# Two small constant tiles moved from the front of SBUF to a place between activations and weight halves

## The chip, the cores and the metric

The kernel runs on one core of a Trainium2 chip. The metric is the device time of one launch in microseconds, as the median of several runs. Inside the core the work is done by TensorE (PE for its matmuls, PEld for its loads of stationary operands), VectorE (DVE), ScalarE (ACT) and GpSimd (POOL), while DMA queues bring the weights from HBM into SBUF, the on-chip memory.

## The reference

The reference is a two-layer decoder trunk over 256 tokens of width 2048, in float32. Layer 0 mixes with multi-head latent attention beside a causal pooling mixer, layer 1 with a gated short convolution, and each layer ends in a squared-ReLU MLP of hidden width 8192:

```python
for layer in range(DEPTH):                     # DEPTH = 2
    h = _rmsnorm(x, mix_norm_g[layer])
    if layer % 2 == 0:
        c_q, c_kv, k_rope, u_pool = jnp.split(h @ even_w_in[e], split_at, axis=-1)
        a = _mla(c_q, c_kv, k_rope, ...)       # 8 heads, causal softmax
        b = _pool_mixer(u_pool, ...)           # trailing means over 2/4/8/16 tokens
        x = x + jnp.concatenate([a, b], axis=-1) @ even_w_out[e]
    else:
        x = x + _short_conv(h, odd_w_in[o], odd_conv_w[o], odd_w_out[o])
    x = x + _mlp(_rmsnorm(x, mlp_norm_g[layer]), w_mlp_up[layer], w_mlp_down[layer])
```

`_mlp(h, w_up, w_down)` is `square(relu(h @ w_up)) @ w_down`.

## The kernel before, in words

**Split operands.** Each float32 matrix product is made of three products of a reduced type: a weight or activation is split into a high part (`hi`) and a low part (`lo`), and `lo * lo` is left out. Weights arrive in blocks of 1 MB (`raw`, 128 partitions by 2048 elements, DMA at L129). `halved` (L132) makes the halves from each block, two tiles of 1024 elements at a time: ScalarE copies `hi` (L141), VectorE subtracts it from the block to give `lo` (L142). Six slots of `hi` and six of `lo` go round.

**Two orders of operands.** TensorE loads one operand first and keeps it (the stationary operand, `lhsT`), then streams the other (the moving operand, `rhs`). The kernel uses both orders:

```python
def columns_out(o, act, kt, w, c0, first, last):          # weights stationary
    hi, lo = w
    nc.tensor.matmul(o, lhsT=hi[:, c0:c0 + P], rhs=act[:, kt, :], start=first, stop=False)          # L161, 512 wide
    nc.tensor.matmul(o[:, S:2 * S], lhsT=lo[:, c0:c0 + P], rhs=act[:, kt, 0:S], start=False, stop=last)  # L162, 256 wide
```

`columns_out` makes the MLP's up projection and the convolution's three gates; its moving operand is always `xT`, the normed activations of the layer. `tokens_out` (L147 to L156) is the other way round: the stationary operand is an activation tile (`hT`, or `xT` in the latent projection at the start) and the moving one a weight half, `hi` at L154, `lo` at L155, `hi` at L156, 512 wide nearly everywhere, 384 and 320 in the latent projection. The lines L777 to L779 inside `down_seven` do the same for a part of the MLP's down projection; their stationary operand is a piece of `hT` or of `fT`, a tile of sums of such pieces. `columns_summed` (L167 to L169) serves the pooling mixer with steps of 256, weights stationary, `xT` moving.

**Stages.** In order: latent and pooling projections and attention of layer 0 (to about 240 us), the MLP of layer 0, the convolution layer (from about 960 us: the gates L911 to L948, all in `columns_out`, then `project_out`), the MLP of layer 1. An MLP starts with two chunks of up projection by themselves. Then `mlp` interleaves up steps with down products in an order written out by hand (L883), fourteen chunks of up projection among seven groups of products, and ends with four blocks of down projection alone (L889). In all there are 2816 pairs of L161 and L162: 768 in the gates, 256 in the opening chunks of the two MLPs, 1792 in the interleaved parts. There are 880 triples of L154 to L156 that are 512 wide, and 392 triples of L777 to L779, of which 168 have `hT` stationary and 224 `fT`.

**Where tiles lie in SBUF.** Pools get their places one after the other from the front, in the order in which the code opens them: `const`, `big` (`x`, `xT`, `qkv`), `small`, `acts` (four activation tiles `hT`), `halves` (twelve slots), then the pools of the stage (`raws`, and `blocks`, `forms` or `conv`). The pool `attn` lies at the far end. All sizes below are bytes in each partition; every tile is rounded up to 32 bytes. In the program before:

| tiles | start of the first | size of one | start modulo 256 |
|---|---|---|---|
| `gains`, `minus_half`, `warm`, `ident` (in `const`) | 16512, 17024, 17152, 17280 | 512, 128, 128, 512 | |
| `x` | 18208 | 16384 | 32 |
| `xT` | 34592 | 32768 | 32 |
| `hT` (four) | 78048 | 8192 | 224 |
| `hi` (six), `lo` (six) | 110816 | 4352 | 224 |
| `raw` (three) | 163040 | 8192 (8704 at first) | 224 |
| `fT` (two) | 204000 | 8192 | 224 |

A slot of `halves` is 4352 bytes, seventeen times 256, so all twelve start at the same place modulo 256 and alternate modulo 512. Inside the tiles the pieces used by matmuls start at multiples of 512 bytes, or of 1024 in `hT`.

**The two tiles of the change.** `minus_half` is 32 columns of -0.5, written once by GpSimd (L248) and read by GpSimd's few power operations (L269, L367, L564, L915). `warm` takes the result of one ScalarE activation (L250) that is there to have the activation table loaded early; nothing reads it.

Of the kernel before, what the change touches and what calls it, by code (L numbers as in the profile page):

```python
# [9 lines left out]
F32 = mybir.dt.float32  # L10
F32R = mybir.dt.float32r
I32 = mybir.dt.int32
AF = mybir.ActivationFunctionType
# [3 lines left out]
P = 128  # L17
# [50 lines left out]
def trunk(ctx: ExitStack, tc, x_in, xT_in, gains_in, pos_in, w_up, w_down, w_in, pool_in, w_uq, w_ukv,  # L68
          qn_g, kn_g, pool_w, w_out, odd_in, odd_out, freq_in, out):
    nc = tc.nc  # L70
    PSUM = bass.MemoryType.PSUM

    const = ctx.enter_context(tc.tile_pool(name="const", bufs=1))
# [14 lines left out]
    small = ctx.enter_context(tc.tile_pool(name="small", bufs=2))  # L88
    T4 = dict(tag="t", bufs=4)
    acts = ctx.enter_context(tc.tile_pool(name="acts", bufs=4))  # L90
    pools = dict(halves=ctx.enter_context(tc.tile_pool(name="halves", bufs=6)))
    psum = ctx.enter_context(tc.tile_pool(name="psum", bufs=4, space=PSUM))

# [150 lines left out]
    for name, n in (("mix0", KD), ("mix1", KD), ("mlp", 2 * KD), ("conv", 3 * KD), ("scale", POOLW // P), ("qa", KL), ("kva", KL)):  # L244
        gains[name] = (gains_t, at)
        at += n
    minus_half = const.tile([P, 32], F32, name="minus_half")
    nc.gpsimd.memset(minus_half, -0.5)  # L248
    warm = const.tile([P, 32], F32, name="warm")
    nc.scalar.activation(warm, minus_half, AF.Square)  # L250
    ident = const.tile([P, P], F32, name="ident")
    make_identity(nc, ident)
    ps_warm = bank2()
# [751 lines left out]
```

## Time and profile before

| | |
|---|---|
| median of 3 runs | 2018.85 us (2018.52 to 2019.94) |
| the profiled execution's own time | 2020.08 us |
| its span, first to last instruction | 2018.3 us |
| mean granted TensorE clock | 0.998 |
| PE busy | 2007.2 us, 99% |
| DVE, ACT, POOL busy | 1394.9, 1122.2, 96.4 us |
| read from HBM | 455.89 MB |

A row of the timeline starts with the time at which an instruction began, counted from the start of the span. For matmuls the time from one start to the next is the step that TensorE took; the duration in the second column is longer, since matmuls are pipelined, and does not count here. Below, a step is always taken as the time between two starts with many steps between them, divided by their number, since starts are shown to 0.01 us.

### The profile page before, as it was taken

What the parts mean: (1) busy time and instruction counts of PE and PEld (TensorE: products, weight loads), DVE (VectorE), ACT (ScalarE), POOL (GpSimd) and SP (SyncE); (2) the same over time, 40 slices, a digit from 0 to 9 for tenths busy, and PEclk for the clock granted to TensorE, in tenths of its full rate; (3) what the DMA queues carried; (4) which work ended last, traced back from release to release, by engine and by line L of the source; (5) the groups of instructions that cost most, each with busy time, mean ns of one, the idle gap of its engine ahead of it and who ended that gap; (6) DMA issues with size and microseconds to landing.
All of it is one profiled execution on the core that took longest, in us unless ns stands there. A gap on an engine that the chain in (4) does not pass through costs nothing.

```text
span 2018.3 us, 26720 instructions
## 1 busy us (share of the span) xinstructions
PE 2007.2 (99%) x10532; PEld 1723.4 (85%) x10532; DVE 1394.9 (69%) x1737; ACT 1122.2 (56%) x1480; POOL 96.4 (5%) x126
## 2 busy tenths in 40 slices
PE   8999999999999999999999999999999999999999
PEld 8988888888888888888888888888888888888887
DVE  6677667777777777676566656567777777767774
ACT  6476556665556555555444444456555566555552
POOL 1330000000000000000000000000000000000000
PEclk9999999999999999999999999999999999999999
DMA  8453758787978878665555557658787977879663
GB/s 312 163 193 141 228 189 231 266 254 251 271 250 271 252 240 276 233 209 188 183 181 187 185 186 245 215 185 244 241 282 243 284 235 265 253 251 286 201 219 125
DMA packets 67006, 459.72 MB, mean 228 GB/s; under 512 B 7280, under 2 KB 9760, under 8 KB 11968
## 3 DMA queue, kind: packets, MB, share of 16 engines
q1 hardware_dynamic: 58224, 397.89, 54.5%
q0 software_dynamic: 8224, 58.94, 15.4%
q8 instruction: 82, 1.34, 0.3%
q10 hardware_dynamic: 432, 1.18, 0.2%
q14 instruction: 44, 0.36, 0.0%
HBM read 455.89 MB, written 2.10 MB: 227 GB/s over the span
## 4 chain that ended last, share of the span: by engine, by line
PE 96%; DVE 1%; POOL 1%; DMA 1%; ACT 1%; issue 0%; SPq 0%; ACTq 0%; DVEq 0%; POOLq 0%
PE ps L161 32%; PE ps L162 16%; PE ps L154 10%; PE ps L156 10%; PE ps L155 10%; PE ps L777 4%; PE ps L779 4%; PE ps L778 4%; DVE lo L142 1%; DMA raw<-in_even_w_in 1%; PE ps L289 1%; PE ps L167 0%; PE ps L169 0%; PE ps L168 0%; POOL pn L489 0%
## 5 line engine op out<-in xcount | busy, mean ns | idle before, releaser
L142 DVE TENSOR_TENSOR lo<-raw,hi 128x1024 fp32r<-128x1024 f32 (+2 forms) x694 | 847.6, 1225 | 444.4 <-ACT hi L141 443.5
L141 ACT CAST hi<-raw 128x1024 fp32r<-128x1024 f32 (+2 forms) x694 | 725.7, 1048 | 613.2 <-PE ps L161 338.1
L161 PE MATMUL ps<-xT,hi 128*128 128x512 f32 x2816 | 992.1, 394 | 0.0
L162 PE MATMUL ps<-xT,lo 128*128 128x256 f32 x2816 | 790.8, 281 | 0.0
L161 PEld LDWEIGHTS ps<-xT,hi 128*128 128x128 f32 x2816 | 529.4, 188 | 123.8
L162 PEld LDWEIGHTS ps<-xT,lo 128*128 128x128 f32 x2816 | 528.0, 188 | 3.6
L154 PE MATMUL ps<-hi,hT 128*128 128x512 f32 (+1 forms) x896 | 349.1, 390 | 0.0
L156 PE MATMUL ps<-hi,hT 128*128 128x512 f32 (+1 forms) x896 | 347.3, 388 | 0.0
L155 PE MATMUL ps<-lo,hT 128*128 128x512 f32 (+1 forms) x896 | 347.1, 387 | 0.0
L154 PEld LDWEIGHTS ps<-hi,hT 128*128 128x128 f32 x896 | 168.3, 188 | 35.0 <-issue 1.3
L156 PEld LDWEIGHTS ps<-hi,hT 128*128 128x128 f32 x896 | 168.3, 188 | 34.8
L155 PEld LDWEIGHTS ps<-lo,hT 128*128 128x128 f32 x896 | 168.4, 188 | 33.2
L141 ACT CAST hi<-t 128x1024 fp32r<-128x1024 f32 x84 | 88.5, 1053 | 92.7 <-PE ps L161 50.7
L142 DVE TENSOR_TENSOR lo<-t,hi 128x1024 fp32r<-128x1024 f32 x84 | 102.6, 1221 | 44.3 <-ACT hi L141 44.1
L767 POOL DMA_DIRECT2D t<-in_w_mlp_down x42 | 36.6, 872 | 1144.4 <-DVE lo L142 682.5
L777 PE MATMUL ps<-hi,fT 128*128 128x512 f32 x224 | 88.1, 393 | 0.0
L779 PE MATMUL ps<-hi,fT 128*128 128x512 f32 x224 | 87.7, 392 | 0.0
L778 PE MATMUL ps<-lo,fT 128*128 128x512 f32 x224 | 87.0, 389 | 0.0
L777 PE MATMUL ps<-hi,hT 128*128 128x512 f32 x168 | 65.8, 392 | 0.0
L779 PE MATMUL ps<-hi,hT 128*128 128x512 f32 x168 | 65.5, 390 | 0.0
L778 PE MATMUL ps<-lo,hT 128*128 128x512 f32 x168 | 65.4, 389 | 0.0
L867 DVE SCALAR_TENSOR_TENSOR x<-ps,r,x 128x512 f32<-128x512 f32 (+1 forms) x73 | 50.9, 737 | 14.5 <-PE ps L156 14.5
(184 smaller groups left out, 1563.9 us busy)
## 6 DMA issues: line engine op xcount, KB each, us to landing
raw<-in_w_mlp_up SPq DMA_DIRECT2D x128, 1024.0 KB, 6.4
raw<-in_w_mlp_down SPq DMA_DIRECT2D x114, 1024.0 KB, 5.2
raw<-in_odd_w_in SPq DMA_DIRECT2D x48, 1024.0 KB, 4.9
t<-in_w_mlp_down POOLq DMA_DIRECT2D x42, 1024.0 KB, 9.7
raw<-in_even_w_out SPq DMA_DIRECT2D x16, 1024.0 KB, 5.0
raw<-in_odd_w_out SPq DMA_DIRECT2D x16, 1024.0 KB, 5.0
t<-in_w_mlp_down SPq DMA_DIRECT2D x14, 1024.0 KB, 5.0
v<-in_w_mlp_down SPq DMA_DIRECT2D x14, 1024.0 KB, 4.9
```

The lines of the kernel that those rows point to most:

```text
L141: a = nc.scalar.copy(h, r)
L142: v = nc.vector.tensor_tensor(out=l, in0=r, in1=h.bitcast(F32), op=ALU.subtract)
L154: nc.tensor.matmul(o, lhsT=a_hi, rhs=hi[:, c0:c0 + n], start=first, stop=False)
L155: nc.tensor.matmul(o, lhsT=a_hi, rhs=lo[:, c0:c0 + n], start=False, stop=False)
L156: nc.tensor.matmul(o, lhsT=a_lo, rhs=hi[:, c0:c0 + n], start=False, stop=last)
L161: nc.tensor.matmul(o, lhsT=hi[:, c0:c0 + P], rhs=act[:, kt, :], start=first, stop=False)
L162: nc.tensor.matmul(o[:, S:2 * S], lhsT=lo[:, c0:c0 + P], rhs=act[:, kt, 0:S], start=False, stop=last)
L767: nc.gpsimd.dma_start(b, at(e, n), accum_op=ALU.add)
L777: nc.tensor.matmul(o, lhsT=a_hi, rhs=hi, start=q == 0, stop=False)
L778: nc.tensor.matmul(o, lhsT=a_hi, rhs=lo, start=False, stop=False)
L779: nc.tensor.matmul(o, lhsT=a_lo, rhs=hi, start=False, stop=q == 3)
L867: nc.vector.scalar_tensor_tensor(out=xb, in0=ps[:, t, :n], scalar=r2[0][:, t:t + 1], in1=xb, op0=ALU.mult, op1=ALU.add)
```

## The change

A pool `back` is opened between `acts` and `halves`, and the two tiles move there from `const`. `warm` shrinks from 32 columns (128 bytes) to 16 (64 bytes), and its activation reads 16 columns.

```diff
     acts = ctx.enter_context(tc.tile_pool(name="acts", bufs=4))
+    back = ctx.enter_context(tc.tile_pool(name="back", bufs=1))
     pools = dict(halves=ctx.enter_context(tc.tile_pool(name="halves", bufs=6)))
...
-    minus_half = const.tile([P, 32], F32, name="minus_half")
+    minus_half = back.tile([P, 32], F32, name="minus_half")
     nc.gpsimd.memset(minus_half, -0.5)
-    warm = const.tile([P, 32], F32, name="warm")
-    nc.scalar.activation(warm, minus_half, AF.Square)
+    warm = back.tile([P, 16], F32, name="warm")
+    nc.scalar.activation(warm, minus_half[:, :16], AF.Square)
```

No other instruction is added, removed or moved in the code.

## The prediction

> **What bounds the kernel now.** I read the page's busy times first, then its chain, then the waits of PE, then the starts of matmuls in the timeline, stage by stage.
>
> ```profile
> PE 2007.2 (99%) x10532; PEld 1723.4 (85%) x10532; DVE 1394.9 (69%) x1737; ACT 1122.2 (56%) x1480; POOL 96.4 (5%) x126
> PEclk9999999999999999999999999999999999999999
> DMA  8453758787978878665555557658787977879663
> PE 96%; DVE 1%; POOL 1%; DMA 1%; ACT 1%; issue 0%; SPq 0%; ACTq 0%; DVEq 0%; POOLq 0%
> ```
>
> TensorE is busy 99% of the span and is 96% of the chain that ended last. DMA, VectorE and ScalarE all have slack. The waits of PE say the same:
>
> ```profile
> PE ps L255 <- POOL ident masks.py:199: 2.5, 1, 2.5
> PE ps L154 <- ACT hi L141: 2.0, 2, 1.1
> PE ps L167 <- ACT qkv L525: 1.6, 1, 1.6
> PE ps L155 <- DVE lo L142: 1.0, 2, 0.9
> PE ps L167 <- DVE hT L205: 0.2, 1, 0.2
> ```
>
> That is 7.3 us of named waits in the whole run. So the time is the sum of matmul steps, and the change, which adds no work, can matter only if steps of matmuls get longer or shorter. What does a step take? The next rows are pairs of starts of the same line, read in order.
>
> ```profile
> 1099.71 0.39 PE L161 MATMUL ps<-xT,hi 128*128 128x512 f32 x1
> 1102.89 0.39 PE L161 MATMUL ps<-xT,hi 128*128 128x512 f32 x1
> ...
> 1600.47 0.40 PE L161 MATMUL ps<-xT,hi 128*128 128x512 f32 x1
> 1611.64 0.39 PE L161 MATMUL ps<-xT,hi 128*128 128x512 f32 x1
> ...
> 1254.77 0.39 PE L154 MATMUL ps<-hi,hT 128*128 128x512 f32 x1
> 1259.53 0.39 PE L154 MATMUL ps<-hi,hT 128*128 128x512 f32 x1
> ...
> 2008.69 0.28 PE L154 MATMUL ps<-hi,hT 128*128 128x256 f32 x1
> 2014.09 0.28 PE L154 MATMUL ps<-hi,hT 128*128 128x256 f32 x1
> ...
> 61.05 0.28 PE L167 MATMUL ps<-xT,hi 128*128 128x256 f32 x1
> 66.35 0.28 PE L167 MATMUL ps<-xT,hi 128*128 128x256 f32 x1
> ```
>
> First two rows, in the gates of the convolution: nine pairs of L161 and L162 lie between them, 3.18 us / 9 = 353.3 ns a pair. Next two, in the interleaved MLP: 32 pairs in 11.17 us, 349.1 ns a pair. Then `tokens_out` in the output projection: 21 steps in 4.76 us, 226.7 ns for a step of 512. The closing steps of 256 in the same function: 45 in 5.40 us, 120.0 ns. Last, `columns_summed`: 45 steps of 256 in 5.30 us, 117.8 ns.
>
> The reader is to see this: 226.7 + 120.0 = 346.7 ns is what a step of 512 and one of 256 cost in `tokens_out`. The same two widths in `columns_out` cost 349.1 or 353.3 ns, 2.4 or 6.6 ns more. Nothing waits there; the loads of stationary operands and the streams just run slightly slower. The granted clock is full in all four stages:
>
> ```profile
> 1000.00:1100.00 100.00, 100.00 (x568) 87.12 (x567) 62.59 (x78) 43.23 (x47) 0.41 (x4) 1.00 0.55 189
> 1400.00:1960.00 560.00, 560.00 (x2858) 476.97 (x2857) 413.11 (x476) 326.91 (x379) 19.86 (x23) 1.00 0.80 253
> 1240.00:1320.00 80.00, 80.00 (x366) 66.42 (x365) 44.64 (x48) 38.52 (x54) 1.77 (x2) 1.00 0.72 242
> 1970.00:2010.00 40.00, 40.00 (x183) 33.34 (x182) 19.99 (x21) 11.61 (x11) 0.00 (x0) 1.00 0.39 139
> ```
>
> (Columns: window, its length, busy us of PE, PEld, DVE, ACT, POOL, granted clock, DMA share, GB/s.) The slow gates have the least ACT and DVE work and a low DMA share, so other engines' traffic is not what lengthens their steps.
>
> A second place shows that a step of one width has two lengths. In the latent projection, sixteen k-tiles follow each other, each with twelve steps of 384 and six of 320:
>
> ```profile
> 13.69 0.34 PE L155 MATMUL ps<-lo,xT 128*128 128x384 f32 x1
> 14.21 0.34 PE L155 MATMUL ps<-lo,xT 128*128 128x384 f32 x1
> ...
> 46.17 0.34 PE L154 MATMUL ps<-hi,xT 128*128 128x384 f32 x1
> 48.25 0.31 PE L154 MATMUL ps<-hi,xT 128*128 128x320 f32 x1
> ...
> 49.13 0.34 PE L154 MATMUL ps<-hi,xT 128*128 128x384 f32 x1
> 51.25 0.31 PE L154 MATMUL ps<-hi,xT 128*128 128x320 f32 x1
> ```
>
> The first pair is in the first k-tile: three steps in 0.52 us, 173.3 ns. The second: twelve in 2.08 us, 173.3 ns. The third, the k-tile after it: twelve in 2.12 us, 176.7 ns. So there is a short step and a long one, 3.4 ns apart, and from about 43 us on they alternate with the k-tile.
>
> **The change part by part.** *The instructions.* One activation reads 16 columns for 32; the write of `minus_half` and all of GpSimd's power operations stay.
>
> ```profile
> L250 ACT ACTIVATE warm<-minus_half x1: 229/229/229, 2.5 to 2.5; 128x32 f32<-128x32 f32 x1
> 2.35 13.03 DMA raw<-in_even_w_in
> ```
>
> The activation takes 229 ns at 2.5 us, under the first weight load, which the chain shows from 2.35 us for 13.03 us. It is worth nothing while that load is there, and at most 0.2 us if it were gone. The change adds no wait and moves no DMA; no queue's order changes. I cost this part at 0.
>
> *The addresses.* `const` loses 256 bytes, so `x`, `xT`, `ident`, `small` and `hT` start 256 lower: the same place modulo 256. `back` gives 128 + 64 = 192 bytes back, so `hi`, `lo`, `raw`, `fT` and what follows start 64 lower: 160 modulo 256 instead of 224. Operands that are both before `back`, or both after it, keep their distance: the transposes with `ident`, VectorE's and ScalarE's passes over `raw`, `hi` and `lo`, and the 224 triples with `fT`. What alters is the distance from the moving operand to the stationary one, modulo 256, wherever one is a weight half and the other is `xT` or `hT`:
>
> - `columns_out`, weights over `xT`: 224 - 32 = 192 before, 160 - 32 = 128 after.
> - `tokens_out` and the triples with `hT`: 0 before, 224 - 160 = 64 after.
> - latent projection, `xT` over weights: 64 before (32 - 224), 128 after.
>
> This lines up with the steps. Distance 0: always the short step (226.7, 120.0). Distance 64 or 192, both odd multiples of 64: 349.1 or 353.3 ns a pair, and long steps in half of the latent k-tiles. I take as theory that the load of the next stationary operand and the running stream get in each other's way in SBUF at odd multiples of 64, and not at even ones. Two rows speak against it: 117.8 ns at distance 192 is shorter than 120.0 at 0, and the first k-tile has the short step at distance 64.
>
> *What it is worth.* In the gates and opening chunks 768 + 256 = 1024 pairs would go from 353.3 to 346.7 ns: 1024 x 6.6 = 6.8 us less. In the interleaved parts 1792 x 2.4 = 4.3 us less. The latent k-tiles with the long step: six of them, 6 x 12 x 3.4 ns = 0.2 us less. Against it, 880 x 3 + 168 x 3 = 3144 steps of 512 go to distance 64, where before shows no step of 512 at all. Bounds: 0 each (the steps of 320 of that distance, and the first k-tile, show nothing extra), and 3.4 ns each (the k-tiles with the long step), together 10.7 us; below nothing only if a step of 512 could be shorter than the 226.7 ns which all of `tokens_out` keeps, and 117.8 against 120.0 leaves that open for the 256-wide ones alone. I take the middle, since the row nearest in shape, 384 wide in the same function at the same distance, has the long step in every second k-tile, and the weight slots will again alternate modulo 512 as they do there: 1572 x 3.4 = 5.3 us more. Sum: -6.8 - 4.3 - 0.2 + 5.3 = -6.0 us. The profiled execution took 2020.08 us around a span of 2018.3; the same 6.0 comes off the median of the runs shown, 2018.85, which is 1.2 below it: 2012.9, say 2013 us.
>
> *A rule that speaks against it.* By the rows above, stages with the same granted clock and nothing awaited differ by up to 6.6 ns a pair. The Trainium skill, page "TensorE: Matmul & The Clock Gate", Part 2, "Step-by-step: what each phase is for", has TensorE read the stream and the next load through two independent SBUF ports, and "Loading the next tile's weights doesn't steal SBUF read bandwidth from the running matmul"; its page "SBUF — State Buffer", "Who interferes with whom", says "PE and ACT never wait on anyone". By that rule no address matters and the sum is 0, which is 2018.85 us. This trace fits it badly where one width has steps of 173.3 and 176.7 ns, but it shows no run with other addresses, so it cannot refute it.
>
> **The rivals.** *No change.* The length of a step hangs on how the stream of matmuls entered its rhythm, not on addresses. For it: the same pair, same tiles, same distance takes 349.1 ns between down products and 353.3 alone, and the first latent k-tile is short where later ones at the same distance are long. Against: the alternation with the slots. Time: 2018.85, within 2 us or so since rhythms may fall otherwise in places.
>
> *Slower.* The steps of `tokens_out` and of the triples with `hT` all take the long step at distance 64, and `columns_out` keeps its rhythm. For it: these 3144 steps are at the shortest length that the trace shows for 512, so they can only lose. Against: half of the latent steps at that distance are short. Time: 2018.85 + 10.7 = 2029.5. It decides against me as soon as the tokens' loss passes the columns' gain: at full loss, when less than 10.7 of 11.3 us is won. If the interleaved pairs also went to 353.3 ns, 1792 x 4.2 = 7.5 us more, 2037.
>
> *More than forecast.* The columns gain all and the tokens lose nothing: 2018.85 - 11.3 = 2007.6. If the 256-wide step also fell to 117.8, 2816 x 2.2 = 6.2 us more, 2001.4.
>
> **How the numbers follow.** About 0.2%, 4 us, is what a measurement of this kernel can tell from no change. The forecast, columns win and tokens lose a part or none, has 0.45, of which 0.15 for the case with no loss; no change 0.30; slower 0.25. These are also the chances of faster, same and slower, since 2013 and 2007.6 lie more than 4 us under 2018.85 and 2029.5 more than 4 us over it. The range goes from 2004, which leaves out the far part of the best case, to 2028, which leaves out about half of the slower case. The forecast's own range is 2005 to 2015.
>
> **What would show it.** Right: in the gates 353.3 ns a pair falls to about 347, in the interleaved MLP 349.1 to about 347, and no wait of PE grows. The steps of 512 in the output projection (226.7) stay in some blocks and go to about 230 in others. The DMA queues, the busy times of ACT and DVE, and the waits keep their size. Wrong: gate pairs stay at 353.3 and token steps at 226.7 (no change), or token steps are 230 throughout while gate pairs stay (slower). If the time moves and all steps keep their lengths, a wait or a dropped granted clock must have moved instead, and the theory is not about the cause at all.

## The result, and the profile after

The changed kernel takes 2036.97 us (median of 4 runs, 2036.71 to 2038.28) against 2018.75 us before in the same comparison: 1.0091 times as long, with an interval of 1.0076 to 1.0106. It is slower by 0.9%, and above the range that was given.

The page of the changed kernel: busy times, granted clock, DMA share by slices, and the chain that ended last.

```profile
PE 2024.6 (99%) x10532; PEld 1724.7 (85%) x10532; DVE 1395.8 (69%) x1737; ACT 1122.3 (55%) x1480; POOL 96.8 (5%) x126
PEclk9999999999999999999999999999999999999999
DMA  8453758787978879665555557558787977879663
PE 96%; DVE 1%; DMA 1%; POOL 1%; ACT 1%; issue 0%; SPq 0%; ACTq 0%; DVEq 0%; POOLq 0%
```

The counts of instructions are those of before, VectorE and ScalarE are busy as long as before to 0.9 us, and the DMA digits differ from before in two of the 40 slices. Only PE is busy longer, by 17.4 us. The waits of PE after the change (engine, line, what it waited for: us in total, times, longest):

```profile
PE ps L256 <- POOL ident masks.py:199: 2.5, 1, 2.5
PE ps L156 <- DVE lo L143: 1.8, 2, 0.9
PE ps L155 <- ACT hi L142: 1.0, 2, 0.6
PE ps L611 <- DVE hT L206: 1.0, 1, 1.0
PE ps L168 <- DVE hT L206: 0.3, 1, 0.3
```

They add up to 6.6 us, against 7.3 before. So no wait is the cause, and the steps are what is left. (All lines of the changed kernel stand one or more further down: L154 of before is L155, L161 is L162, L777 is L778.) First the last blocks of the second MLP's down projection, in `tokens_out`, in the timeline of before:

```profile
1983.53 0.39 PE L154 MATMUL ps<-hi,hT 128*128 128x512 f32 x1
2007.33 0.39 PE L154 MATMUL ps<-hi,hT 128*128 128x512 f32 x1
```

Between these starts lie 105 steps of 512: 23.80 us / 105 = 226.7 ns. The same instructions in the timeline after the change, then 30 pairs of the gates, then 32 pairs of the interleaved MLP:

```profile
1999.71 0.40 PE L155 MATMUL ps<-hi,hT 128*128 128x512 f32 x1
2024.21 0.39 PE L155 MATMUL ps<-hi,hT 128*128 128x512 f32 x1
...
1103.78 0.40 PE L162 MATMUL ps<-xT,hi 128*128 128x512 f32 x1
1114.32 0.40 PE L162 MATMUL ps<-xT,hi 128*128 128x512 f32 x1
...
1438.27 0.39 PE L162 MATMUL ps<-xT,hi 128*128 128x512 f32 x1
1449.51 0.40 PE L162 MATMUL ps<-xT,hi 128*128 128x512 f32 x1
```

The step in `tokens_out` is now 24.50 / 105 = 233.3 ns, 6.6 ns longer. A pair of the gates takes 10.54 / 30 = 351.3 ns (353.3 before), and a pair of the interleaved MLP 11.24 / 32 = 351.3 ns in these rows; over all of the interleaved pairs the mean is 350.7 ns (349.2 before).

Could work of another engine, or a DMA, lengthen the steps? Near the end of each trace lies a stretch of some 3 us in which nothing but TensorE and its loads is busy. Before, then after (window, its length, busy us of PE, PEld, DVE, ACT, POOL, granted clock, DMA share, GB/s):

```profile
2000.40:2003.40 3.00, 3.00 (x15) 2.49 (x14) 0.00 (x0) 0.00 (x0) 0.00 (x0) 1.00 0.00 0
```

```profile
2017.00:2020.20 3.20, 3.20 (x15) 2.61 (x14) 0.00 (x0) 0.00 (x0) 0.00 (x0) 1.00 0.00 0
```

Twelve steps inside the first take 2.72 us, 226.7 ns each, and twelve inside the second 2.80 us, 233.3 ns each. The long step is there with all other engines and the DMA queues idle, so their work does not cause it; what is left is TensorE's own operands.

The triples of `down_seven` hold a control inside one line: with `hT` stationary the distance changed from 0 to 64, with `fT` it did not. The groups of that line, before and then after (us busy in all, mean ns of one):

```profile
L777 PE MATMUL ps<-hi,fT 128*128 128x512 f32 x224 | 88.1, 393 | 0.0
L777 PE MATMUL ps<-hi,hT 128*128 128x512 f32 x168 | 65.8, 392 | 0.0
```

```profile
L778 PE MATMUL ps<-hi,fT 128*128 128x512 f32 x224 | 87.7, 392 | 0.0
L778 PE MATMUL ps<-hi,hT 128*128 128x512 f32 x168 | 66.6, 396 | 0.0
```

The `fT` matmuls of this line keep their duration (393 and 392 ns), those with `hT` go from 392 to 396. What the triples cost in all is in the next table.

Adding up the times from each matmul's start to the next one's over both whole traces accounts for the difference:

| steps | count | before, us | after, us | difference |
|---|---|---|---|---|
| `tokens_out`, 512 wide | 2640 | 601.5 | 617.9 | +16.4 |
| triples with `hT` | 504 | 115.0 | 117.6 | +2.6 |
| triples with `fT` | 672 | 153.9 | 154.2 | +0.3 |
| pairs of `columns_out` | 5632 | 987.8 | 988.3 | +0.5 |
| all others | 1082 | 153.6 | 150.3 | -3.3 |
| sum | 10530 | 2011.7 | 2028.3 | +16.6 |

The spans differ by the same 2034.9 - 2018.3 = 16.6 us. The +0.5 of the pairs is +2.6 in the 1792 interleaved ones and -2.1 in the 1024 others. The -3.3 lies for the most part in the first 200 us, and part of it is not the change's. The windows there, before and then after (the column behind the busy times of POOL is the granted clock):

```profile
0.00:100.00 100.00, 94.43 (x652) 93.15 (x653) 61.50 (x122) 56.34 (x93) 25.02 (x43) 0.98 0.66 240
100.00:200.00 100.00, 98.16 (x522) 82.80 (x521) 74.01 (x148) 67.41 (x185) 21.11 (x18) 0.98 0.47 169
```

```profile
0.00:100.00 100.00, 94.72 (x662) 93.69 (x663) 62.86 (x123) 57.63 (x94) 25.43 (x43) 1.00 0.66 240
100.00:200.00 100.00, 98.68 (x519) 81.45 (x518) 73.74 (x153) 67.46 (x186) 21.11 (x18) 1.00 0.47 169
```

The profiled execution of before had 0.98 of the clock in these 200 us, that of the changed kernel 1.00. The first experiment below, whose trace has 1.00 there and the distances of before, gives an estimate of what this is worth: about 2.2 us, so that the change itself comes to 18.8 us of span, beside 18.2 between the medians.

### The profile page after: what moved, and what is told of

It reads as the page before. It is cut to its first block, busy times and chain, and to the rows that moved or that the text cites. A ratio compares the mean times of both kernels' runs of the same rounds, so it can differ in the third digit from the quotient of the medians.

```text
span 2034.9 us, 26720 instructions
## 1 busy us (share of the span) xinstructions
PE 2024.6 (99%) x10532; PEld 1724.7 (85%) x10532; DVE 1395.8 (69%) x1737; ACT 1122.3 (55%) x1480; POOL 96.8 (5%) x126
## 4 chain that ended last, share of the span: by engine, by line
PE 96%; DVE 1%; DMA 1%; POOL 1%; ACT 1%; issue 0%; SPq 0%; ACTq 0%; DVEq 0%; POOLq 0%
PE ps L162 32%; PE ps L163 17%; PE ps L155 10%; PE ps L156 10%; PE ps L157 10%; PE ps L778 4%; PE ps L780 4%; PE ps L779 4%; DVE lo L143 1%; DMA raw<-in_even_w_in 1%; PE ps L290 1%; POOL pn L490 0%; PE ps L168 0%; PE ps L169 0%; PE ps L170 0%
## 5 line engine op out<-in xcount | busy, mean ns | idle before, releaser
L162 PE MATMUL ps<-xT,hi 128*128 128x512 f32 x2816 | 992.6, 394 | 0.0
L162 PEld LDWEIGHTS ps<-xT,hi 128*128 128x128 f32 x2816 | 528.8, 188 | 121.7
L155 PE MATMUL ps<-hi,hT 128*128 128x512 f32 (+1 forms) x896 | 354.2, 395 | 0.0
L156 PE MATMUL ps<-lo,hT 128*128 128x512 f32 (+1 forms) x896 | 352.3, 393 | 0.0
L157 PE MATMUL ps<-hi,hT 128*128 128x512 f32 (+1 forms) x896 | 352.2, 393 | 0.0
L155 PEld LDWEIGHTS ps<-hi,hT 128*128 128x128 f32 x896 | 168.3, 188 | 40.3 <-issue 1.3
L778 PE MATMUL ps<-hi,fT 128*128 128x512 f32 x224 | 87.7, 392 | 0.0
L778 PE MATMUL ps<-hi,hT 128*128 128x512 f32 x168 | 66.6, 396 | 0.0
```

Of the source, the lines that this page charges most:

```text
L155: nc.tensor.matmul(o, lhsT=a_hi, rhs=hi[:, c0:c0 + n], start=first, stop=False)
L156: nc.tensor.matmul(o, lhsT=a_hi, rhs=lo[:, c0:c0 + n], start=False, stop=False)
L157: nc.tensor.matmul(o, lhsT=a_lo, rhs=hi[:, c0:c0 + n], start=False, stop=last)
L778: nc.tensor.matmul(o, lhsT=a_hi, rhs=hi, start=q == 0, stop=False)
```

## The experiments

All kernels but the first come from the kernel before by one edit: `minus_half` gets 64 columns, so that `const` keeps its size without `warm`, and a padding tile goes behind `acts` (pool `back`, kernels named p), ahead of `acts` (pool `front`, kernels named q), or both (kernels named tok). A pad behind `acts` moves the weight halves and so changes the distance (start of the stationary operand minus start of the moving one, modulo 256) in `tokens_out` and in `columns_out`. A pad ahead of `acts` moves `hT` along, so that `tokens_out` keeps its distance and `columns_out` changes (with it the short loops at the start that read `xT`: the latent projection and `columns_summed`). The pads, of N bytes in each partition:

```diff
# p64, p128, p32 (N = 64, 128, 32)
     acts = ctx.enter_context(tc.tile_pool(name="acts", bufs=4))
+    back = ctx.enter_context(tc.tile_pool(name="back", bufs=1))
...
-    minus_half = const.tile([P, 32], F32, name="minus_half")
+    minus_half = const.tile([P, 64], F32, name="minus_half")
     nc.gpsimd.memset(minus_half, -0.5)
-    warm = const.tile([P, 32], F32, name="warm")
-    nc.scalar.activation(warm, minus_half, AF.Square)
+    warm = back.tile([P, N // 4], F32, name="warm")
+    nc.scalar.activation(warm, minus_half[:, :N // 4], AF.Square)
```

```diff
# q64, q192, q32, q224, q96, q160 (N as in the name); minus_half as above
+    front = ctx.enter_context(tc.tile_pool(name="front", bufs=1))
     acts = ctx.enter_context(tc.tile_pool(name="acts", bufs=4))
...
+    warm_f = front.tile([P, N // 4], F32, name="warm_f")
+    nc.scalar.activation(warm_f, minus_half[:, :N // 4], AF.Square)
# tok64: warm_f of 64 bytes and warm of 192; tok32: warm_f of 64 and warm of 224
```

Each kernel with its two distances, its time and its ratio to the kernel before in the same comparison (2018.75 us for the change, and 2018.29 us for all64 to q64, 2018.40 for tok64 to q224, 2018.14 for p32 to q160). Behind them stand the mean steps, worked out from the starts of such matmuls in its trace without the few long ones where a loop is interrupted (in `tokens_out` 21 of 2640 are over 250 ns in every trace; with them its means are 0.7 ns longer):

| kernel | distance tokens | distance columns | us | ratio | tokens step, ns | gates pair, ns | interleaved pair, ns |
|---|---|---|---|---|---|---|---|
| before | 0 | 192 | 2018.75 | | 227.1 | 353.3 | 349.2 |
| after | 64 | 128 | 2036.97 | 1.0091 [1.0076, 1.0106] | 233.3 | 351.2 | 350.7 |
| all64 | 0 | 192 | 2018.61 | 1.0002 [0.9993, 1.0011] | 227.1 | 353.3 | 349.2 |
| p64 | 192 | 0 | 2029.93 | 1.0059 [1.0044, 1.0074] | 229.0 | 353.3 | 352.1 |
| p128 | 128 | 64 | 2041.41 | 1.0118 [1.0101, 1.0135] | 232.4 | 353.4 | 352.9 |
| q64 | 0 | 0 | 2020.10 | 1.0011 [1.0002, 1.0020] | 227.0 | 347.3 | 352.7 |
| tok64 | 64 | 192 | 2036.82 | 1.0084 [1.0069, 1.0099] | 233.4 | 353.3 | 349.2 |
| q192 | 0 | 128 | 2019.78 | 1.0006 [0.9997, 1.0015] | 227.1 | 351.2 | 350.3 |
| q32 | 0 | 224 | 2007.59 | 0.9942 [0.9925, 0.9958] | 227.1 | 346.8 | 347.6 |
| q224 | 0 | 160 | 2018.38 | 0.9998 [0.9989, 1.0007] | 227.1 | 350.2 | 350.5 |
| p32 | 224 | 224 | 2024.87 | 1.0037 [1.0023, 1.0050] | 233.2 | 346.8 | 347.6 |
| tok32 | 32 | 224 | 2025.28 | 1.0036 [1.0023, 1.0049] | 233.2 | 346.8 | 347.5 |
| q96 | 0 | 32 | 2014.85 | 0.9985 [0.9975, 0.9994] | 227.2 | 353.3 | 347.1 |
| q160 | 0 | 96 | 2007.88 | 0.9947 [0.9931, 0.9964] | 226.9 | 346.8 | 347.3 |

**Is it the distance, or the places themselves?** all64 moves everything behind `const` by 64 bytes, which keeps the distances between all these tiles and puts the weight halves at 160 modulo 256, where the change puts them:

```diff
-    warm = const.tile([P, 32], F32, name="warm")
-    nc.scalar.activation(warm, minus_half, AF.Square)
+    warm = const.tile([P, 16], F32, name="warm")
+    nc.scalar.activation(warm, minus_half[:, :16], AF.Square)
```

> All tiles behind ident start 64 bytes lower (warm shrinks to 64 bytes inside const, no pool back). Weight halves lie at 160 modulo 256 as after the change, but every distance between operands is that of before (0 for tokens_out, 192 for columns_out). Theory 'distance' (a step's length follows from the start of the stationary operand less that of the moving one, modulo 256): as before, 2018.8 us within 2, steps of 512 in tokens_out 226.7 to 227.1 ns, gate pairs 353.3. Rival 'own place' (the weight halves' own start modulo 256 counts): as after, about 2037, steps of 233.3 ns. Rival 'rhythm' (any shift redraws the lengths): neither, somewhere between 2005 and 2040.

Measured: 2018.61 us, no change. Its timeline, thirty pairs of the gates and the same 105 steps of `tokens_out` as above, then twelve steps of a latent k-tile:

```profile
1094.31 0.39 PE L161 MATMUL ps<-xT,hi 128*128 128x512 f32 x1
1104.91 0.39 PE L161 MATMUL ps<-xT,hi 128*128 128x512 f32 x1
...
1981.32 0.39 PE L154 MATMUL ps<-hi,hT 128*128 128x512 f32 x1
2005.12 0.39 PE L154 MATMUL ps<-hi,hT 128*128 128x512 f32 x1
...
47.40 0.34 PE L154 MATMUL ps<-hi,xT 128*128 128x384 f32 x1
49.48 0.31 PE L154 MATMUL ps<-hi,xT 128*128 128x320 f32 x1
```

353.3 ns and 226.7 ns, as before. So the place of the weight halves modulo 256 does not matter by itself. Added up like the table above, each of its first four rows agrees with before to 0.02 us; only the others are 2.2 us shorter, and its granted clock in the first 200 us is the changed kernel's:

```profile
0.00:100.00 100.00, 95.35 (x669) 94.31 (x670) 63.43 (x123) 58.06 (x95) 24.94 (x43) 1.00 0.66 240
100.00:200.00 100.00, 97.11 (x515) 81.22 (x515) 73.89 (x154) 66.94 (x185) 21.13 (x18) 1.00 0.49 169
```

Its span is 2016.1 us. Against that trace the change is +16.4 +2.6 +0.3 +0.5 in the table's rows and -1.0 in the others, 18.8 us.

The last two rows of the timeline are of the fifteenth k-tile, which took 176.7 ns a step in the kernel before (its rows, from 49.13 us, stand in the prediction) and takes 2.08 us / 12 = 173.3 here. Though all addresses were moved alike, the long and short k-tiles have changed places. Which k-tile is the long one therefore does not follow from its slot's address.

**A pad behind the activations.** p64 and p128 go through further distances with the same move as the change.

> A pad of 64 bytes between activations and halves, the front as before: distance 192 in tokens_out, 0 in columns_out. Theory 'distance', with one table for both functions (512 wide: 226.7 at 0, 233.3 at 64, 230.6 at 128, 230.3 to 233.5 at 192; 256 wide: 120.0 at 0, 113.0 at 64, 119 to 120 at 128, 117.8 to 119 at 192): columns_out pairs at 346.7 ns (11.3 us less), tokens_out and hT triples at about 231 ns (3144 x 4 ns = 12.6 us more), together about 2020 us. 'Own place': no forecast for 32 modulo 256. 'Rhythm': columns_out pairs keep 349 and 353.

Measured: 2029.93 us. Its timeline, gates and then `tokens_out`:

```profile
1101.12 0.40 PE L162 MATMUL ps<-xT,hi 128*128 128x512 f32 x1
1111.72 0.40 PE L162 MATMUL ps<-xT,hi 128*128 128x512 f32 x1
...
1993.57 0.39 PE L155 MATMUL ps<-hi,hT 128*128 128x512 f32 x1
2017.61 0.39 PE L155 MATMUL ps<-hi,hT 128*128 128x512 f32 x1
```

353.3 ns for a pair at distance 0, and 24.04 us / 105 = 229.0 ns for a step at 192, where the change's 64 gives 233.3. The 11.3 us that the pairs were to win did not come: over the whole trace they take 5.1 us more than before, and so does `tokens_out`.

> A pad of 128 bytes between activations and halves: distance 128 in tokens_out, 64 in columns_out. Theory 'distance' with the same table: columns_out pairs at 233.3 + 113.0 = 346.3 ns (about 12 us less), tokens_out and hT triples at 230.6 ns (3144 x 3.6 = 11.3 us more), together about 2018 us. If the table differs between the two functions (which operand streams matters), columns_out pairs stay at 349 to 353 and the time is about 2030. 'Rhythm': no fixed relation.

Measured: 2041.41 us, the slowest of all. Its `tokens_out`, at distance 128:

```profile
2003.02 0.39 PE L155 MATMUL ps<-hi,hT 128*128 128x512 f32 x1
2027.42 0.39 PE L155 MATMUL ps<-hi,hT 128*128 128x512 f32 x1
```

24.40 us / 105 = 232.4 ns. An even multiple of 64 gives a step nearly as long as an odd one does: the order that the prediction assumed is refuted for `tokens_out`. Adding up all starts as for the change gives +14.0 us for `tokens_out`, +2.8 for the `hT` triples, +0.3 for `fT`, +6.7 for the pairs and, against all64, -1.5 for the others, together 22.3 us, beside 23.1 between the medians.

**A pad ahead of the activations, columns alone.**

> A pad of 64 bytes ahead of the activation tiles, none behind: hT and the weight halves move together, distance 0 in tokens_out as before, and 0 in columns_out. Theory 'distance' with one table: tokens_out stays at 226.7 to 227.1 ns, columns_out pairs at 226.7 + 120.0 = 346.7 ns in the gates and in the interleaved MLP, 1024 x 6.6 + 1792 x 2.5 = 11.2 us less: about 2007.6 us. If columns_out has a table of its own, 2015 to 2025. 'Rhythm': tokens_out changes as well.

Measured: 2020.10 us. Its gates, at distance 0 as in p64:

```profile
1097.54 0.39 PE L162 MATMUL ps<-xT,hi 128*128 128x512 f32 x1
1107.94 0.39 PE L162 MATMUL ps<-xT,hi 128*128 128x512 f32 x1
```

10.40 us / 30 = 346.7 ns, where p64 has 353.3 for the same instructions at the same distance of their own operands. So a pair's length does not follow from that distance alone. The same shows inside q64: the opening chunks of both MLPs, the same function at the same distance, keep 353.3 ns a pair. The interleaved pairs got longer at the same time (349.2 to 352.7), and that took the gain back: 768 x 6.0 ns = 4.6 us less in the gates, 1792 x 3.5 ns = 6.3 us more in the interleaved parts. The difference, 1.7 us, is that of the medians, 1.8.

**The two parts of the change apart.** tok64 has the change's distance in `tokens_out` and the old one in `columns_out`; q192 the reverse.

> One part of the change alone: pads of 64 bytes ahead of the activation tiles and 192 behind them, so that tokens_out and the hT triples have distance 64 as after the change, while columns_out keeps 192 as before (the weight halves are 256 bytes further on). Theory 'distance, each function by itself': 2640 steps x 6.3 ns + 504 x 5.3 ns = 19.2 us more than before, about 2037.5 us; columns_out pairs as before, 353.3 ns in the gates and 349.2 in the interleaved MLP. Rival 'entry': a changed rhythm of tokens_out changes the rhythm in which columns_out starts, so that pairs leave 349.2 and 353.3 and the time is off by up to 2816 x 4 ns = 11 us.

Measured: 2036.82 us, as slow as the change (one of its four runs, not the profiled one, took 2032.46). Gates, then `tokens_out`:

```profile
1103.44 0.40 PE L163 MATMUL ps<-xT,hi 128*128 128x512 f32 x1
1114.04 0.40 PE L163 MATMUL ps<-xT,hi 128*128 128x512 f32 x1
...
1999.09 0.39 PE L156 MATMUL ps<-hi,hT 128*128 128x512 f32 x1
2023.59 0.39 PE L156 MATMUL ps<-hi,hT 128*128 128x512 f32 x1
```

353.3 ns as before, and 233.3 ns as after the change. The `fT` triples, moved by 256 together with the weights, take 153.9 us in all as before, those with `hT` 117.9 for 115.0. The pairs of `columns_out`, whose distance grew by exactly 256, take 987.7 us in all against 987.8: a period of 256 shows here.

> The other part alone: a pad of 192 bytes ahead of the activation tiles, none behind, so that columns_out has distance 128 as after the change and tokens_out keeps 0. Theory 'distance, each function by itself': pairs as in the changed kernel, 351.2 ns in the gates (1024 x 2.1 = 2.1 us less with the opening chunks) and 350.7 interleaved (1792 x 1.5 = 2.7 us more), tokens_out 227.1: about 2018.9 us, no measurable change. Rival 'entry': pairs differ from those of the changed kernel, since they are entered from steps of another length.

Measured: 2019.78 us, 1.0006, whose interval includes 1. Gates, then `tokens_out`:

```profile
1096.24 0.39 PE L162 MATMUL ps<-xT,hi 128*128 128x512 f32 x1
1106.78 0.39 PE L162 MATMUL ps<-xT,hi 128*128 128x512 f32 x1
...
1983.47 0.39 PE L155 MATMUL ps<-hi,hT 128*128 128x512 f32 x1
2007.27 0.39 PE L155 MATMUL ps<-hi,hT 128*128 128x512 f32 x1
```

351.3 ns as after the change, 226.7 ns as before it. The two halves of the change are separate, and the whole loss is in `tokens_out` and the `hT` triples.

**Distances that are no multiple of 64.** The remaining kernels shift the weights by odd multiples of 32.

> A pad of 32 bytes ahead of the activation tiles: tokens_out keeps distance 0, columns_out gets 224, a value between those seen. Theory 'distance': tokens_out 227.1 ns; columns_out between its values at 192 and 0, so 349 to 353 ns a pair: 2015 to 2025 us. If only multiples of 64 matter, as at 192: 2018.3. All weight blocks also start at a multiple of 256 for the DMA; if that mattered for the time, DMAs would land earlier and the waits of ACT for raw would shrink, without a change in the end time since TensorE is the bound.

Measured: 2007.59 us, 0.9942, faster than both kernels. Its busy times, then thirty pairs of the gates and 32 of the interleaved MLP:

```profile
PE 1995.7 (99%) x10532; PEld 1725.2 (86%) x10532; DVE 1394.2 (69%) x1737; ACT 1122.9 (56%) x1480; POOL 96.5 (5%) x126
```

```profile
1090.00 0.39 PE L162 MATMUL ps<-xT,hi 128*128 128x512 f32 x1
1100.40 0.39 PE L162 MATMUL ps<-xT,hi 128*128 128x512 f32 x1
...
1419.10 0.40 PE L162 MATMUL ps<-xT,hi 128*128 128x512 f32 x1
1430.21 0.39 PE L162 MATMUL ps<-xT,hi 128*128 128x512 f32 x1
```

346.7 and 347.2 ns, about the 346.7 that the prediction hoped for at 128. Over the whole trace the pairs take 978.4 us, 9.4 less than before, of the 10.8 us between the medians.

> A pad of 224 bytes ahead of the activation tiles: tokens_out keeps distance 0, columns_out gets 160, between 128 and 192. Theory 'distance': tokens_out 227.1 ns, pairs 349 to 353 ns: 2015 to 2025 us. 'Entry': gates and opening chunks jump between about 347 and 353 ns a pair with no order in the distance.

Measured: 2018.38 us, no change: a pair of the gates became 3.1 ns shorter, one of the interleaved parts 1.3 ns longer.

> A pad of 32 bytes behind the activation tiles: distance 224 in both functions. Theory 'distance, each function by itself': columns_out as with 32 bytes ahead of the activations (347.0 ns in the gates, 347.6 interleaved, 10.8 us less); tokens_out at 224 is new: at best 226.7 as at 0 (2007.6 us in all), at worst about 233 (3144 x 6 ns = 19 us more, 2027). If one table serves both functions, a step of 512 at 224 is 228.5 ns as in columns_out: 3144 x 1.5 = 4.7 us more than 2007.6, 2012.3.

Measured: 2024.87 us. The columns are as short as in q32, but `tokens_out` is at 224:

```profile
1987.50 0.40 PE L155 MATMUL ps<-hi,hT 128*128 128x512 f32 x1
2012.01 0.39 PE L155 MATMUL ps<-hi,hT 128*128 128x512 f32 x1
```

24.51 us / 105 = 233.4 ns. The same distance, 224, is short for pairs of `columns_out` and long for steps of `tokens_out`.

> Pads of 64 bytes ahead of and 224 behind the activation tiles: columns_out at 224 as in the best kernel so far, tokens_out at 32. Theory 'distance, each function by itself': pairs at 347.0 and 347.6 ns; the step of 512 at 32 is new, between its values at 0 (227.1) and 64 (233.4): 2007.6 to 2027 us. If it is shorter than at 0, this kernel is below 2007.6.

Measured: 2025.28 us, with 233.2 ns in `tokens_out` at 32. Of the six distances seen there, 0 alone has the short step.

> A pad of 96 bytes ahead of the activation tiles: tokens_out keeps 0, columns_out gets 32. Theory 'distance': tokens_out 227.1 ns; pairs between their values at 0 (352.7 and 347.3) and 64 (352.9 and 353.4): 2008 to 2021 us. If the odd multiples of 32 are short as 224 is, pairs at about 347 and 2007.6 us.

Measured: 2014.85 us. The interleaved pairs are short (347.1 ns) and the gates are not (353.3), the reverse of q64.

> A pad of 160 bytes ahead of the activation tiles: tokens_out keeps 0, columns_out gets 96. Theory 'distance': tokens_out 227.1 ns; pairs between their values at 64 (352.9 and 353.4) and 128 (350.7 and 351.2): about 2021 us. If the odd multiples of 32 are short as 224 is, pairs at about 347 and 2007.6 us; 160, which gave 350.4, speaks against that.

Measured: 2007.88 us, 0.9947, all pairs short. Its time cannot be told from q32's.

## Why the prediction was wrong

**Right.** The time is the sum of TensorE's steps: the differences of starts give the whole 16.6 us between the spans, and no wait grew. The instructions of the change cost nothing. What acts is the distance between stationary and moving operand: all64 keeps it and changes nothing, tok64 changes it in `tokens_out` and the `hT` triples alone and gives the whole effect, and the `fT` triples stand still beside `hT` triples of the same line. VectorE and ScalarE are as busy as before to 0.9 us. The rival of no change, that lengths hang on rhythm and not on addresses, falls by the same runs, but only as a rule for everything: q64 against p64, and the latent k-tiles of all64, show that for pairs and latent steps something beside the distance counts as well.

**The step that failed** is the price of the tokens term. The prediction bounded 3144 steps by 0 and 3.4 ns each, from latent steps 384 wide, and took half: 5.3 us. Measured are 6.2 ns on 2640 steps of `tokens_out` and 5.2 on 504 with `hT`, together 19.0 us, nearly twice the upper bound. The bound was none: it came from another width and from steps that were themselves not all at their shortest (173.3 and 176.7 ns, and 175.9 to 176.5 after the change). And the half came from the alternation with the slots, which all64 shows not to follow the slots' addresses; at distance 64 all blocks of `tokens_out` have the long step. The case that it named for this was the slower rival, right in its mechanism and short in its price.

**The second wrong step** is the sign by even and odd multiples of 64. The columns term, -6.8 and -4.3 us, came to +0.5: -2.1 in the gates and opening chunks, where 353.3 ns fell to 351.2 and not to 346.7, and +2.6 in the interleaved parts, where 349.2 rose to 350.7. The small latent term, -0.2, had the wrong sign too: where k-tiles of 173.3 and 176.7 ns took turns, now those of 175.9 and 176.5 do. For `tokens_out`, p128 shows 232.4 ns at an even multiple. The idea that pairs of `columns_out` take the step of `tokens_out` at a good distance is right in its size (346.8 ns in q32 and q160) and wrong in the distance at which it holds.

The time that it named in the slower rival for further mishaps, 2037, was met by other terms: not by interleaved pairs of 353.3 ns, but by steps of 512 that grew by 6.2.

**One reading was wrong.** The prediction says that the gates have the least VectorE and ScalarE work. Its own rows give VectorE 63% there against 56% and 50% in the two stretches of `tokens_out`, and ScalarE 43% against 48% and 29%. That other engines do not lengthen the steps does not follow from those rows; the stretch after the change in which they are all idle shows it for `tokens_out`.

**The rule that spoke against it.** The step of 512 in `tokens_out` grew from 226.7 to 233.3 ns at a granted clock of 1.00 with nothing awaited, by a move of operands alone. The rule of two independent ports in the Trainium skill, page "TensorE: Matmul & The Clock Gate", Part 2, "Step-by-step: what each phase is for", from which the prediction worked out no change, does not agree with the time of a matmul in these runs. Whether the ports themselves are independent, no run here shows.

**What stays open.** Why the distance acts. A conflict between the load of the next stationary operand and the stream would fit the data, as that is what has a distance, but no run takes the one without the other, and the recorded loads of `tokens_out` last 188 ns before and after. The lengths have no order in the distance, and two functions have different orders. For pairs the distance does not settle everything: at 192, 128 and 224 kernels that differ in `tokens_out` have the same pairs (to 0.1 ns in the gates and 0.4 interleaved), but at 0 p64 and q64 do not. These runs give a table for this kernel, not a rule.

## What to carry to other kernels

In a kernel that is bound by back-to-back matmuls, each with a load of its own, take the step of every loop from starts in the trace, before and after any edit that moves pools, even if it moves nothing but constants: here 32 to 224 bytes of padding were worth -0.6% to +1.2%. Padding ahead of one operand's pool in pieces of 32 bytes is a cheap search, and the loops can be read separately in one run. A row of another width is no bound for the price of a step.

## What the runs showed of the hardware that was not expected

- A 512-wide fp32r step in `tokens_out` takes 226.9 to 227.2 ns at distance 0 and 229.0 to 233.4 at 32, 64, 128, 192 and 224, on average over each trace as in the table.
- A pair of `columns_out` takes from 346.8 to 353.4 ns, and `columns_out` is shortest at 96 and 224, where `tokens_out` at 224 takes 233.2.
- The same pairs at the same distance 0 take 353.3 ns in the gates of p64 and 347.3 in those of q64, which differ in the distance of `tokens_out`, and in q96 gates and interleaved pairs differ by 6.2 ns at one distance.
- A shift by 256 bytes of `columns_out`'s weights changes nothing (987.7 against 987.8 us in all).
- The steps of 384 in the latent projection (`xT` stationary, distance taken in the same way) go by their own distance. From the fifth k-tile on they take 175.7 ns at 0 (p64, q64) and 173.3 at 32 (q32, p32, tok32); at 64 (before, all64, tok64) k-tiles of about 173.4 and 176.7 take turns, at 128 (the change, q192) k-tiles of about 175.9 and 176.5. Whether the k-tiles take turns goes with the distance; which one is long does not.
